# A relative attention bias laid out from 32 shifted lines a head in place of 128, and read as 256 columns in place of 384

## The chip, the cores and the metric

The kernel runs on one core of one Trainium2 chip. The metric is the device time of one execution in microseconds (us); lower is better. Five engines work side by side, each through its own instructions in order: TensorE (PE in the profile; its weight loads are listed as PEld), VectorE (DVE), ScalarE (ACT), GpSimd (POOL) and SyncE (SP), which here issues all the DMA transfers.

## The reference

One step of a two-layer streaming encoder for 256 prompt frames and 32 sample frames of width 1024. Only the start of layer 0 matters here. Half of its 16 heads (group A, 8 heads of size 64) attend to their own chunk of 64 frames and those before it, with a learned bias a head that depends on the clipped distance of query and key:

```python
def rel_bias_table(rel_bias, q_loc, k_loc):
    rel = jnp.clip(q_loc[:, None] - k_loc[None, :], -REL_CLIP, REL_CLIP) + REL_CLIP
    return jnp.moveaxis(rel_bias[rel].astype(jnp.float32), -1, 0)

def band_attend(q, k, v, bias, valid=None):
    s = jnp.einsum('bqhd,bkhd->bhqk', q, k).astype(jnp.float32) * (HEAD_DIM ** -0.5) + bias
    if valid is not None:
        s = jnp.where(valid, s, NEG_INF)
    p = jax.nn.softmax(s, axis=-1)
    return jnp.einsum('bhqk,bkhd->bqhd', p.astype(v.dtype), v)
```

The other eight heads (group B) use stick-breaking attention without a bias. Then follow the output projection, cross-attention into 256 memory rows, a SwiGLU block, and layer 1 with 16 forgetting-attention heads and the same two blocks.

## The kernel before

Activations lie with features on the partitions: eight tiles of 128 features by 288 tokens (256 prompt, 32 sample). A weight matrix comes in blocks of 128x1024, 512 KB each. `unit` loads one into `st` (a pool of four), ScalarE casts it to a high part `hi`, and VectorE subtracts to get the low part `lo`; `project` then runs 24 matmuls of 288 columns into one accumulator `pj`, three for each of the eight feature tiles: `hh` by `hi`, `hl` by `hi`, `hh` by `lo`. A projection can thus begin when `hi` is cast but needs `lo` from its third matmul on.

Layer 0's mixing (`mix_ab`) goes over eight pairs of heads, j = 0 to 7. For each pair it projects q, k and v in this order; I call them q0, k0, v0, q1 and so on. VectorE takes each out of its accumulator, scaled by `rstd` (`evac_q`, line 718; `evac_kv`, line 725), and k and v are also stored to memory (the transfer `kv<-kv`, line 726). Pairs 0 to 3 are group A. After v of a pair, `attend_prompt` (line 357) transposes v (`vt`), makes the scores (`sc`), runs `softmax` on VectorE and ScalarE (`e`), transposes the weights (`tp`, copied out as `pt`) and multiplies by v (`po`). After odd pairs the sample frames of two pairs are attended to as well (`ss`, `es`, `ts`, `os`).

The bias of a head is a line of 384 numbers, and query p reads it shifted by p. After q0, `rel_lines` (line 729) writes the eight lines to memory and copies each 128 times with a stride of 385 into `skew`; read back with a stride of 384, row p is the line shifted by p. `rel_prompt` (line 749) fetches a head's bias as a tile `bi` of 128x384: 128 columns for the first 128 queries against the first 128 keys, 256 for the second 128 queries against all 256, and fills the future chunk's two corners with a large negative number. `rel_sample` (line 757) fetches 32 rows of 160 columns for each of four heads (`bs`).

The Python order of the code isn't the order on the engines. A scheduler places each instruction on its engine's queue when it expects its inputs and buffers to be there, and from then on the queue is fixed: SP issues its transfers in that order, and one that waits for its data stands in front of those behind it. Transfers also take turns on eight completion semaphores, so that each waits for the one eight places ahead of it to have landed.

Of the kernel before, what the change touches and what calls it, by code (L numbers as in the profile page):

```python
# [8 lines left out]
F32 = mybir.dt.float32  # L9
# [6 lines left out]
P = 128  # L16
NT = 288
NP = 256
NS = 32
KT = 8  # L20
NEG = -1e30
# [5 lines left out]
def encoder_step(ctx: ExitStack, tc: tile.TileContext, a):  # L27
# [13 lines left out]
    dr = ctx.enter_context(tc.tile_pool(name="dr", bufs=1, space=bass.MemoryType.DRAM))  # L41
    V, S, G, T, DMA = nc.vector, nc.scalar, nc.gpsimd, nc.tensor, nc.sync
    cnt = [0]

    def name(s):
        cnt[0] += 1
        return f"{s}{cnt[0]}"

    def tok(s, dt=F32):
        return tk.tile([P, NT], dt, tag="t", name=name(s))  # L50

    def work(s):
        return wk.tile([P, 512], F32, tag="w", name=name(s))
# [4 lines left out]
    def small(s):  # L58
        return sm.tile([P, 8], F32, tag="s", name=name(s))
# [4 lines left out]
    def att(s):  # L64
        return ps.tile([P, 512], F32, tag="at", bufs=4, name=name(s))

    def mm(out, lhsT, rhs, start=True, stop=True):
        T.matmul(out, lhsT, rhs, start=start, stop=stop, skip_group_check=True)  # L68
# [82 lines left out]
    def project(src, h, n=NT, w=None, begun=None):  # L151
        if begun:
            w, p = begun
        else:
            w, p = w or unit(src), acc("pj")
        with tc.issue_after(warmed.ins):
            for k in range(BEGIN if begun else 0, KT):
                mm3(p[:, :n], w, k, h, k, k == 0, k == KT - 1)
        tick()
        return p  # L160
# [167 lines left out]
    def v_natural(v):  # L328
        p = att("vt")
        T.transpose(p[:, 0:128], v[:, 0:128], ident)  # L330
        T.transpose(p[:, 128:256], v[:, 128:256], ident)
        T.transpose(p[0:NS, 256:384], v[:, 256:288], ident)
        vn = wk.tile([P, 384], F32, tag="vn", bufs=5, name=name("vn"))
        S.copy(vn[:, 0:256], p[:, 0:256])
        S.copy(vn[0:NS, 256:384], p[0:NS, 256:384])
        return vn

    def softmax(s, cols, bias, out):

        n, rows = len(cols), out.shape[0]  # L340
        st = small("st")[0:rows]
        for i, (c0, c1) in enumerate(cols):
            mx, sm = st[:, i:i + 1], st[:, n + i:n + i + 1]
            if bias is None:
                V.tensor_reduce(mx, s[:, c0:c1], axis=mybir.AxisListType.X, op=ALU.max, negate=True)
                S.activation(out[:, c0:c1], s[:, c0:c1], AF.Exp, bias=mx, accum_out=sm)
            else:
                V.tensor_tensor_reduce(out=out[:, c0:c1], in0=s[:, c0:c1], in1=bias[:, c0:c1], scale=-1.0, scalar=3e38,
                                       op0=ALU.add, op1=ALU.min, accum_out=mx)
                S.activation(out[:, c0:c1], out[:, c0:c1], AF.Exp, bias=mx, scale=-1.0, accum_out=sm)  # L350
        V.reciprocal(st[:, 2 * n:3 * n], st[:, n:2 * n])
        for i, (c0, c1) in enumerate(cols):
            V.tensor_scalar(out[:, c0:c1], out[:, c0:c1], st[:, 2 * n + i:2 * n + i + 1], None, op0=ALU.mult)

    QT = [(0, 128), (128, 384)]

    def attend_prompt(q, k, v, vns, j, bias, oh, ol):

        vn = vns[j] = v_natural(v)
        e = []  # L360
        for hd in range(2):
            r = slice(64 * hd, 64 * hd + 64)
            s = att("sc")
            mm(s[:, 0:128], q[r, 0:128], k[r, 0:128])
            mm(s[:, 128:384], q[r, 128:256], k[r, 0:256])
            e.append(work("e"))
            softmax(s, QT, bias[hd], e[hd])
        yield 1
        w = []
        for hd in range(2):  # L370
            t = att("tp")
            T.transpose(t[:, 0:128], e[hd][:, 0:128], ident)
            T.transpose(t[:, 128:256], e[hd][:, 128:256], ident)
            T.transpose(t[:, 256:384], e[hd][:, 256:384], ident)
            w.append(work("pt"))
            S.copy(w[hd][:, 0:384], t[:, 0:384])
        yield 1
        prompt_pv(w, vn, oh, ol)

    def prompt_pv(w, vn, oh, ol):  # L380
        po = att("po")
        for hd in range(2):
            r = slice(64 * hd, 64 * hd + 64)
            mm(po[r, 0:256], vn[:, 64 * hd:64 * hd + 64], w[hd][:, 0:256], True, False)
            mm(po[r, 128:256], vn[:, 128 + 64 * hd:192 + 64 * hd], w[hd][:, 256:384], False, True)
        split_o(po[:, 0:256], oh[:, 0:256], ol[:, 0:256])
# [329 lines left out]
    def evac_q(cur, p):  # L716
        t = tok("q")
        cur.then(lambda: V.scalar_tensor_tensor(t, p[:, :NT], 0.125, cur.r, op0=ALU.mult, op1=ALU.mult))
        return t

    def evac_kv(cur, p, dst):
        t = tok("kv")

        def go():
            V.tensor_tensor(t, p[:, :NT], cur.r, ALU.mult)
            DMA.dma_start(dst, t)

        cur.then(go)
        return t

    def rel_lines():


        ln = cst.tile([8, 384], F32, name="line")
        DMA.dma_start(ln[:, 128:384], a["rel"][:, 0:256])
        V.tensor_copy(ln[:, 0:128], ln[:, 128:129].to_broadcast([8, 128]))
        d = dr.tile([8, 384], F32, name="lined")
        DMA.dma_start(d, ln)
        sk = dr.tile([8, 128 * 385], F32, name="skew")
        for h in range(8):  # L740
            DMA.dma_start(bass.AP(tensor=sk.tensor, offset=sk.offset + h * 128 * 385, ap=[[385, P], [1, 384]]),
                          bass.AP(tensor=d.tensor, offset=d.offset + 384 * h, ap=[[0, P], [1, 384]]))
        return sk

    def rel_rows(sk, h, c, rows, n):

        return bass.AP(tensor=sk.tensor, offset=sk.offset + h * 128 * 385 + c, ap=[[384, rows], [1, n]])

    def rel_prompt(sk, h):
        t = wk.tile([P, 384], F32, tag="bi", bufs=5, name=name("bi"))  # L750
        DMA.dma_start(t[:, 0:128], rel_rows(sk, h, 256, P, 128))
        DMA.dma_start(t[:, 128:384], rel_rows(sk, h, 128, P, 256))
        G.memset(t[0:64, 64:128], NEG)
        G.memset(t[0:64, 320:384], NEG)
        return t

    def rel_sample(sk, g):
        t = wk.tile([P, 384], F32, tag="bi", bufs=5, name=name("bs"))
        for h in range(4):
            DMA.dma_start(t[32 * h:32 * h + 32, 0:160], rel_rows(sk, 4 * g + h, 128, NS, 160))  # L760
        return t

    def mix_ab(cur, nxt, memory, w0):
        o = ([tok("oh", F32R) for _ in range(KT)], [tok("ol", F32R) for _ in range(KT)])
        qs, ks, vs, vns = {}, {}, {}, {}
        w = a["w_ab"]

        def proj(j):
            b = 12 * (j // 4) + j % 4
            kv = 8 * (j // 4) + j % 4  # L770
            qs[j] = evac_q(cur, project(w[b], cur.h, w=w0 if j == 0 else None))
            if j == 0:
                proj.line = rel_lines()
            ks[j] = evac_kv(cur, project(w[b + 4], cur.h), a["kv0"][kv])
            vs[j] = evac_kv(cur, project(w[b + 8], cur.h), a["kv0"][kv + 4])

        def attend(j):
            args = (qs[j], ks[j], vs[j], vns, j)
            if j < 4:
                return attend_prompt(*args, [rel_prompt(proj.line, 2 * j + i) for i in range(2)], o[0][j], o[1][j])  # L780
            return stick_prompt(*args, o[0][j], o[1][j])

        def sample(g):
            two = (2 * g, 2 * g + 1)
# [249 lines left out]
```

## Time and profile before

| what | value |
|---|---|
| median of 3 runs | 981.52 us (979.58 to 983.31) |
| the profiled execution | 981.77 us, span 979.9 us |
| TensorE busy, share of the span | 960.9 us, 98% |
| VectorE, ScalarE, GpSimd busy | 589.5, 483.8, 194.6 us |
| copies `skew<-lined` | 8 issues of 192 KB, 13.7 to 18.7 us, 6.5 us to landing |
| bias reads `bi<-skew` | 8 of 64 KB and 8 of 128 KB, 20.1 to 49.9 us |
| sample bias reads `bs<-skew` | 8 of 20 KB |

Busy time is the union of an engine's instructions. The bias is read in the first 50 us only, so the span's averages say little about it; the rows of that stretch count. In the timeline a row has start, duration, engine, line, operation, output and inputs, count, and in brackets the idle time ahead with what ended it. In the rows by stretch there are, after the stretch's bounds and length, the busy times of PE, PEld, DVE, ACT and POOL, then the granted TensorE clock, the DMA share and GB/s. A wait row names who waited and for whom, with the total, the count and the longest.

### The profile page before, as it was taken

Reading aid. Unit: us, or ns where it says so; the run is one execution under the profiler, and the core shown is the slowest. Engines: PE = TensorE matmul, PEld = TensorE weight load, DVE = VectorE, ACT = ScalarE, POOL = GpSimd, SP = SyncE. Lnnn points to the kernel's source line nnn. Section 1 sums busy time; section 2 is a strip of 40 time slices with the busy share of each in tenths; the row PEclk is TensorE's granted clock in tenths of the full one; section 3 lists DMA queues with packets and bytes.
Section 4 is the critical chain, followed back from the end, with each engine's and each line's share of the span. In section 5 each row is a group of like instructions: output and inputs, shape, how many; then the busy total and the mean of one; then the engine's idle time right before and its main releaser. Section 6 shows DMA issues by size and latency. Waiting matters only on the chain.

```text
span 979.9 us, 19034 instructions
## 1 busy us (share of the span) xinstructions
PE 960.9 (98%) x7449; PEld 925.1 (94%) x7449; DVE 589.5 (60%) x1135; ACT 483.8 (49%) x854; POOL 194.6 (20%) x293
## 2 busy tenths in 40 slices
PE   8999999999999999999999999999999999999995
PEld 7789999998899999999998999999989999999995
DVE  6686454677676555764565666657757655555452
ACT  5556767555455444444444545445546544444330
POOL 3121001210113222411003234213002222222010
PEclk9999999999999999999999999999999999999997
DMA  7775345544254454455455555545425444444431
GB/s 235 247 248 192 127 165 174 169 168 143 91 179 158 165 173 167 178 193 173 166 201 167 179 191 182 170 160 194 149 100 168 155 159 165 173 164 166 165 109 49
DMA packets 60137, 163.59 MB, mean 167 GB/s; under 512 B 8160, under 2 KB 21520, under 8 KB 60048
## 3 DMA queue, kind: packets, MB, share of 16 engines
q1 hardware_dynamic: 60048, 162.38, 49.0%
q8 instruction: 59, 0.97, 0.4%
q14 instruction: 30, 0.25, 0.1%
HBM read 152.20 MB, written 11.72 MB: 167 GB/s over the span
## 4 chain that ended last, share of the span: by engine, by line
PE 90%; DMA 3%; DVE 3%; issue 1%; ACT 1%; SPq 0%; POOL 0%; DVEq 0%; ACTq 0%; POOLq 0%
PE pj L68 50%; PE dn L68 14%; PE op L68 11%; PE mv L68 5%; DMA st<-w_ab 2%; PE zb L68 1%; PE xs L68 1%; PE xo L68 1%; PE po L68 1%; DVE lo L142 1%; DMA skew<-lined 1%; PE sc L68 1%; PE nr L68 1%; ACT hi L141 1%; PE zs L68 1%
## 5 line engine op out<-in xcount | busy, mean ns | idle before, releaser
L141 ACT CAST hi<-st 128x1024 fp32r<-128x1024 f32 x260 | 272.2, 1049 | 339.4 <-issue 146.9
L68 PE MATMUL pj<-hh,hi 128*128 128x288 f32 (+1 forms) x1352 | 405.1, 300 | 0.0
L68 PE MATMUL pj<-hl,hi 128*128 128x288 f32 (+1 forms) x1352 | 399.8, 296 | 1.7 <-DVE hl L248 1.7
L142 DVE TENSOR_TENSOR lo<-st,hi 128x1024 fp32r<-128x1024 f32 x260 | 323.3, 1244 | 128.8 <-PE dn L68 41.3
L68 PE MATMUL pj<-hh,lo 128*128 128x288 f32 (+1 forms) x1352 | 399.4, 295 | 0.0
L68 PEld LDWEIGHTS pj<-hh,hi 128*128 128x128 f32 x1352 | 256.6, 190 | 6.2 <-issue 4.7
L68 PEld LDWEIGHTS pj<-hl,hi 128*128 128x128 f32 x1352 | 256.5, 190 | 3.3 <-DVE hl L248 3.2
L68 PEld LDWEIGHTS pj<-hh,lo 128*128 128x128 f32 x1352 | 256.7, 190 | 0.0
L68 PE MATMUL dn<-fh,hi 128*128 128x288 f32 x400 | 108.7, 295 | 0.0
L68 PE MATMUL dn<-fh,lo 128*128 128x288 f32 x352 | 103.7, 295 | 0.0
L68 PE MATMUL dn<-fl,hi 128*128 128x288 f32 x304 | 89.5, 294 | 0.0
L68 PE MATMUL op<-ol,hi 128*128 128x288 f32 x256 | 75.5, 296 | 0.0
L68 PE MATMUL op<-oh,lo 128*128 128x288 f32 x256 | 75.5, 295 | 0.0
L68 PE MATMUL op<-oh,hi 128*128 128x288 f32 x256 | 75.1, 296 | 0.0
L68 PEld LDWEIGHTS dn<-fh,hi 128*128 128x128 f32 x400 | 72.5, 188 | 0.0
L68 PEld LDWEIGHTS dn<-fh,lo 128*128 128x128 f32 x352 | 66.1, 188 | 0.0
L213 POOL TENSOR_TENSOR ssq<-ssq,sq 128x288 f32<-128x288 f32 (+1 forms) x37 | 37.0, 1000 | 120.0 <-ACT sq L202 77.8
L68 PEld LDWEIGHTS dn<-fl,hi 128*128 128x128 f32 x304 | 57.1, 188 | 0.0
L691 POOL TENSOR_TENSOR fl<-us,fh 128x288 fp32r<-128x288 f32 x38 | 32.8, 863 | 119.0 <-ACT fh L690 119.0
L686 DVE TENSOR_TENSOR us<-pj,rstd 128x288 f32<-128x288 f32 x44 | 20.1, 457 | 59.4 <-PE pj L68 59.4
L687 POOL TENSOR_TENSOR gs<-gs,sg 128x288 f32<-128x288 f32 x44 | 38.8, 882 | 75.5 <-ACT sg L685 75.5
L68 PEld LDWEIGHTS op<-ol,hi 128*128 128x128 f32 x256 | 48.2, 188 | 0.8 <-issue 0.8
(253 smaller groups left out, 1213.7 us busy)
## 6 DMA issues: line engine op xcount, KB each, us to landing
st<-w_gate SPq DMA_DIRECT2D x44, 512.0 KB, 3.3
st<-w_up SPq DMA_DIRECT2D x44, 512.0 KB, 3.2
st<-w_down SPq DMA_DIRECT2D x44, 512.0 KB, 3.3
st<-w_c SPq DMA_DIRECT2D x25, 512.0 KB, 3.3
st<-w_ab SPq DMA_DIRECT2D x23, 512.0 KB, 4.2
st<-w_xk SPq DMA_DIRECT2D x16, 512.0 KB, 3.6
st<-w_xv SPq DMA_DIRECT2D x16, 512.0 KB, 3.5
st<-w_xq SPq DMA_DIRECT2D x16, 512.0 KB, 4.3
```

The lines of the kernel that those rows point to most:

```text
L68: T.matmul(out, lhsT, rhs, start=start, stop=stop, skip_group_check=True)
L141: S.copy(hi[:, b], st[:, b])
L142: V.tensor_tensor(lo[:, b], st[:, b], hi[:, b].bitcast(F32), ALU.subtract)
L213: eng.tensor_tensor(s[:, :self.n], self.acc[i][:, :self.n], q[:, :self.n], ALU.add)
L686: V.tensor_tensor(us, pu[:, :NT], cur.r, ALU.mult)
L687: G.tensor_tensor(gs, gs, sg, ALU.mult)
L691: G.tensor_tensor(lo, us, hi.bitcast(F32), ALU.subtract)
```

## The change

The shifted copies are made for 32 rows a head, by two transfers of four heads in place of eight of one. A head's bias is fetched by four transfers of 32 rows and 256 columns, each from a start 32 further left in the line. The tile then holds only the 256 columns of the second 128 queries; the first 128 queries use columns 128 to 255 of the same tile, since the same distances stand there, and one corner is filled in place of two.

```diff
-    def softmax(s, cols, bias, out):
+    def softmax(s, cols, bias, out, at=None):
...
-                V.tensor_tensor_reduce(out=out[:, c0:c1], in0=s[:, c0:c1], in1=bias[:, c0:c1], scale=-1.0, scalar=3e38,
+                b0 = at[i] if at else c0
+                V.tensor_tensor_reduce(out=out[:, c0:c1], in0=s[:, c0:c1], in1=bias[:, b0:b0 + c1 - c0], scale=-1.0, scalar=3e38,
...
-        sk = dr.tile([8, 128 * 385], F32, name="skew")
-        for h in range(8):
-            DMA.dma_start(bass.AP(tensor=sk.tensor, offset=sk.offset + h * 128 * 385, ap=[[385, P], [1, 384]]),
-                          bass.AP(tensor=d.tensor, offset=d.offset + 384 * h, ap=[[0, P], [1, 384]]))
+        sk = dr.tile([8, SKEW], F32, name="skew")
+        for h in range(0, 8, 4):
+            DMA.dma_start(bass.AP(tensor=sk.tensor, offset=sk.offset + h * SKEW, ap=[[SKEW, 4], [385, NS], [1, 384]]),
+                          bass.AP(tensor=d.tensor, offset=d.offset + 384 * h, ap=[[384, 4], [0, NS], [1, 384]]))
...
+    SKEW = NS * 385
+
+    def rel_rows(sk, h, c, n):
+
+        return bass.AP(tensor=sk.tensor, offset=sk.offset + h * SKEW + c, ap=[[384, NS], [1, n]])
...
     def rel_prompt(sk, h):
         t = wk.tile([P, 384], F32, tag="bi", bufs=5, name=name("bi"))
-        DMA.dma_start(t[:, 0:128], rel_rows(sk, h, 256, P, 128))
-        DMA.dma_start(t[:, 128:384], rel_rows(sk, h, 128, P, 256))
-        G.memset(t[0:64, 64:128], NEG)
-        G.memset(t[0:64, 320:384], NEG)
+        for p in range(0, P, NS):
+            DMA.dma_start(t[p:p + NS, 0:256], rel_rows(sk, h, 128 - p, 256))
+        G.memset(t[0:64, 192:256], NEG)
         return t
...
-                return attend_prompt(*args, [rel_prompt(proj.line, 2 * j + i) for i in range(2)], o[0][j], o[1][j])
+                return attend_prompt(*args, [rel_prompt(proj.line, 2 * j + i) for i in range(2)], o[0][j], o[1][j], (128, 0))
```

The scheduler then places the neighbours of these instructions anew, on all five queues, between the copies and about 70 us into the program; behind that the queues are as before. In the names below, numbers only tell tiles apart, and they differ by a few between the two kernels.

On SP, from v1's weights (`st_508`) to the store of k1 (`kv_505`), before; `st_568` is q2's weights, `kv_344` and `kv_385` are k0 and v0:

```order
L136 DMA st_508<-w_ab 128x1024
L751 DMA bi_549<-skew 128x128
L752 DMA bi_549<-skew 128x256
L726 DMA kv<-kv_344 128x288
L726 DMA kv<-kv_385 128x288
L751 DMA bi_554<-skew 128x128
L752 DMA bi_554<-skew 128x256
L502 DMA ca_559<-cab 128x512
L502 DMA ca_561<-cab 128x512
L760 DMA bs_563<-skew 32x160 x4
L136 DMA st_568<-w_ab 128x1024
L726 DMA kv<-kv_505 128x288
```

and now, where `st_504` is v1's weights, `st_566` q2's, `kv_501` k1 and `kv_542` v1:

```order
L727 DMA kv<-kv_338 128x288
L727 DMA kv<-kv_379 128x288
L756 DMA bi_382<-skew 32x256 x4
L756 DMA bi_388<-skew 32x256 x4
L727 DMA kv<-kv_501 128x288
L136 DMA st_504<-w_ab 128x1024
L756 DMA bi_545<-skew 32x256 x4
L756 DMA bi_551<-skew 32x256 x4
L503 DMA ca_557<-cab 128x512
L503 DMA ca_559<-cab 128x512
L727 DMA kv<-kv_542 128x288
L136 DMA st_566<-w_ab 128x1024
```

The stores of k0 and v0 moved ahead of the first bias reads, v1's weights moved behind the store of k1, and q2's weights, with k2's and v2's behind them, moved behind the store of v1. (Between the last `ca` and `kv_542` stand four reads of `bs` as before.)

On VectorE, the softmax of pair 0 before (`e_439` and `e_451` are its two heads; `kv_505`, k1, came after both):

```order
L142 TENSOR_TENSOR lo_511<-st_508,hi_510 128x1024
L348 ISA e_439,st_440<-sc_436,bi_388 128x128
L348 ISA st_440 128x1
L348 ISA e_439,st_440<-sc_436,bi_388 128x256
L348 ISA st_440 128x1
L348 ISA e_451,st_452<-sc_448,bi_393 128x128
L348 ISA st_452 128x1
L348 ISA e_451,st_452<-sc_448,bi_393 128x256
L348 ISA st_452 128x1
L351 RECIPROCAL st_440<-st_440 128x2
```

and now:

```order
L726 TENSOR_TENSOR kv_501<-pj_464,rstd_374 128x288
L349 ISA e_435,st_436<-sc_432,bi_382 128x128
L349 ISA st_436 128x1
L349 ISA e_435,st_436<-sc_432,bi_382 128x256
L349 ISA st_436 128x1
L352 RECIPROCAL st_436<-st_436 128x2
L354 TENSOR_SCALAR e_435<-e_435,st_436 128x128
L354 TENSOR_SCALAR e_435<-e_435,st_436 128x256
L349 ISA e_447,st_448<-sc_444,bi_388 128x128
```

k1's evacuation moved ahead of the softmax, and the second head begins only when the first is scaled; v1's low part comes after both.

On TensorE, the end of pair 1's scores for the sample frames before, with k2's projection (`pj_661`) behind it:

```order
L68 MATMUL ss_638<-ca_559,q_460 32x128
L68 MATMUL ss_638<-kv_505,q_460 32x32
L68 MATMUL pj_661<-hh_166,hi_657 128x288
L68 MATMUL pj_661<-hl_167,hi_657 128x288
L68 MATMUL pj_661<-hh_166,lo_658 128x288
```

and now, with q2's projection (`pj_572`) two matmuls into it:

```order
L68 MATMUL ss_636<-kv_501,q_456 32x32
L373 MATMUL tp_692<-ident,e_615 128x128
L374 MATMUL tp_692<-ident,e_615 128x128
L375 MATMUL tp_692<-ident,e_615 128x128
L373 MATMUL tp_698<-ident,e_627 128x128
L374 MATMUL tp_698<-ident,e_627 128x128
L375 MATMUL tp_698<-ident,e_627 128x128
L400 MATMUL ts_704<-ident,es_645 128x128
L401 MATMUL ts_704<-ident,es_645 32x128
L68 MATMUL po_752<-pt_696,vn_609 64x256
L68 MATMUL po_752<-pt_696,vn_609 64x128
L68 MATMUL pj_572<-hh_166,hi_568 128x288
```

Before, q2 stood ahead of the scores and k2 between scores and transposes; now q2, k2 and v2 stand together behind the transposes.

More of the change, by code (lines that the diff above doesn't have):

```diff
@@ L355, in encoder_step, with attend_prompt @@
     QT = [(0, 128), (128, 384)]
-    def attend_prompt(q, k, v, vns, j, bias, oh, ol):
+    def attend_prompt(q, k, v, vns, j, bias, oh, ol, at=None):
         vn = vns[j] = v_natural(v)
@@ L366, in attend_prompt @@
             e.append(work("e"))
-            softmax(s, QT, bias[hd], e[hd])
+            softmax(s, QT, bias[hd], e[hd], at)
         yield 1
@@ L738, in rel_lines @@
         DMA.dma_start(d, ln)
-        sk = dr.tile([8, 128 * 385], F32, name="skew")
-        for h in range(8):
-            DMA.dma_start(bass.AP(tensor=sk.tensor, offset=sk.offset + h * 128 * 385, ap=[[385, P], [1, 384]]),
-                          bass.AP(tensor=d.tensor, offset=d.offset + 384 * h, ap=[[0, P], [1, 384]]))
-        return sk
-    def rel_rows(sk, h, c, rows, n):
-        return bass.AP(tensor=sk.tensor, offset=sk.offset + h * 128 * 385 + c, ap=[[384, rows], [1, n]])
+        sk = dr.tile([8, SKEW], F32, name="skew")
+        for h in range(0, 8, 4):
+            DMA.dma_start(bass.AP(tensor=sk.tensor, offset=sk.offset + h * SKEW, ap=[[SKEW, 4], [385, NS], [1, 384]]),
+                          bass.AP(tensor=d.tensor, offset=d.offset + 384 * h, ap=[[384, 4], [0, NS], [1, 384]]))
+        return sk
+    SKEW = NS * 385
+    def rel_rows(sk, h, c, n):
+        return bass.AP(tensor=sk.tensor, offset=sk.offset + h * SKEW + c, ap=[[384, NS], [1, n]])
     def rel_prompt(sk, h):
         t = wk.tile([P, 384], F32, tag="bi", bufs=5, name=name("bi"))
-        DMA.dma_start(t[:, 0:128], rel_rows(sk, h, 256, P, 128))
-        DMA.dma_start(t[:, 128:384], rel_rows(sk, h, 128, P, 256))
-        G.memset(t[0:64, 64:128], NEG)
-        G.memset(t[0:64, 320:384], NEG)
+        for p in range(0, P, NS):
+            DMA.dma_start(t[p:p + NS, 0:256], rel_rows(sk, h, 128 - p, 256))
+        G.memset(t[0:64, 192:256], NEG)
         return t
@@ L759, in rel_sample @@
         for h in range(4):
-            DMA.dma_start(t[32 * h:32 * h + 32, 0:160], rel_rows(sk, 4 * g + h, 128, NS, 160))
+            DMA.dma_start(t[32 * h:32 * h + 32, 0:160], rel_rows(sk, 4 * g + h, 128, 160))
         return t
```

## The prediction

> **What bounds the kernel now.** I read the page first: the engine totals and the chain of work that ended last.
>
> ```profile
> PE 960.9 (98%) x7449; PEld 925.1 (94%) x7449; DVE 589.5 (60%) x1135; ACT 483.8 (49%) x854; POOL 194.6 (20%) x293
> ...
> PE 90%; DMA 3%; DVE 3%; issue 1%; ACT 1%; SPq 0%; POOL 0%; DVEq 0%; ACTq 0%; POOLq 0%
> ```
>
> TensorE is busy for 98% of the span and carries 90% of the chain, so a change is worth what it adds to or takes from TensorE's idle time. The DMA share of the chain is small and lies in the first 60 us, where the bias is made and read. So the next view is the engines' busy time between 17 us, when the projections run evenly, and 66 us, when the last of the eight biased heads has been transposed:
>
> ```profile
> 17.00:66.00 49.00, 46.36 (x371) 41.76 (x371) 34.77 (x101) 24.30 (x61) 7.03 (x21) 1.00 0.80 251
> ```
>
> The first number after the length is TensorE: 46.36 of 49.00 us. It idles 2.6 us there, and that is the most the change can give back: 981.5 - 2.6 = 978.9 us. The loss has no such limit, and the rest of the argument is about it.
>
> **What the weights wait for.** All transfers leave through SP, in its order. The timeline of SP:
>
> ```profile
> 13.65 5.05 SPq L741 DMA_DIRECT2D skew<-lined  x8
> ...
> 23.37 0.96 SPq L136 DMA_DIRECT2D st<-w_ab  x1
> ...
> 25.41 0.82 SPq L726 DMA_DIRECT2D kv<-kv  x2
> ...
> 28.76 1.82 SPq L760 DMA_DIRECT2D bs<-skew  x4
> 30.68 0.37 SPq L136 DMA_DIRECT2D st<-w_ab  x1
> 34.04 0.36 SPq L726 DMA_DIRECT2D kv<-kv  x1
> 34.49 0.38 SPq L525 DMA_DIRECT2D mem<-memT  x1
> 34.96 0.88 SPq L136 DMA_DIRECT2D st<-w_ab  x2
> ```
>
> The weights at 23.37 are v1's (the value projection of head pair 1), those at 30.68 q2's, the two at 34.96 k2's and v2's. They run ahead of the work: v1's weights leave 8 us before k1's projection has ended. The row at 34.04 is k1's result being stored; SP had nothing out for 3 us before it, and the three loads behind it follow at its heels. A store that waits for its data holds up what stands behind it.
>
> ```profile
> 28.47 0.40 PE L68 MATMUL pj<-hh,hi 128*128 128x288 f32 x1
> ...
> 31.62 0.29 PE L68 MATMUL pj<-hh,lo 128*128 128x288 f32 x1
> ...
> 33.53 0.30 PE L372 MATMUL tp<-ident,e 128*128 128x128 f32 x1 [0.27 <-DVE e L353]
> ...
> 33.89 0.38 PE L68 MATMUL pj<-hh,hi 128*128 128x288 f32 x1
> ...
> 37.27 0.88 PE L68 MATMUL po<-pt,vn 128*64 128x256 f32 x8
> ...
> 53.65 0.40 PE L68 MATMUL pj<-hh,hi 128*128 128x288 f32 x1
> ```
>
> This is TensorE before the change: k1 from 28.47 to 31.62 (24 matmuls, so 0.133 us from start to start), the softmax transposes, v1 from 33.89, the first value product at 37.27, and q3 at 53.65, after q2, k2 and v2. From q3 on the order is nearly the old one, so q3's start is where I read off the sum.
>
> **The change part by part.** Traffic: six of eight shifted copies go, at 5.05/8 = 0.63 us each 3.8 us of SP's time. The reads of the bias go from 16 issues to 32; at the 28.76 row's rate (1.82/4 = 0.46 us for transfers of 32 rows) the 16 more cost 7.4 us of SP's time. Eight fills of 64x64 on POOL go; POOL is busy 7.03 of the 49 us, so nothing is counted. The softmax reads its bias elsewhere in the tile and is otherwise the same, so nothing either. The wait that disappears:
>
> ```profile
> SPq L751 <- DMA skew<-lined: 1.9, 2, 1.4
> ```
>
> It was SP's, not TensorE's. What takes its place is in the order: with the copies finished early, the scheduler has put v1's weights behind the store of k1, and q2's, k2's and v2's weights behind the store of v1. The durations I need:
>
> ```profile
> 28.45 1.05 ACT L141 CAST hi<-st 128x1024 fp32r<-128x1024 f32 x1 [3.92 <-DMA st<-w_ab]
> ...
> 40.63 1.05 ACT L141 CAST hi<-st 128x1024 fp32r<-128x1024 f32 x1 [2.05 <-DMA st<-w_ab]
> ...
> 43.01 1.05 ACT L141 CAST hi<-st 128x1024 fp32r<-128x1024 f32 x1 [1.01 <-DMA st<-w_ab]
> ```
>
> ```profile
> 24.94 0.81 DVE L725 TENSOR_TENSOR kv<-pj,rstd 128x288 f32<-128x288 f32 x2
> ...
> 29.53 1.23 DVE L142 TENSOR_TENSOR lo<-st,hi 128x1024 fp32r<-128x1024 f32 x1 [1.68 <-ACT hi L141]
> 30.67 0.28 DVE L348 CUSTOM_DVE_ANT_0 e<-sc,bi 128x128 f32<-128x128 f32 x1
> ...
> 32.02 0.17 DVE L351 RECIPROCAL st<-st 128x2 f32<-128x2 f32 x1 [0.15 <-ACT e L350]
> 32.22 0.55 DVE L353 TENSOR_SCALAR e<-e,st 128x128 f32<-128x128 f32 x2
> ```
>
> ```profile
> st<-w_gate SPq DMA_DIRECT2D x44, 512.0 KB, 3.3
> ...
> st<-w_ab SPq DMA_DIRECT2D x23, 512.0 KB, 4.2
> ...
> bs<-skew SPq DMA_DIRECT2D x8, 20.0 KB, 3.7
> ```
>
> Nothing before k1's last matmul at 31.62 hangs on the change: its weights leave before the copies. From there, in the new order:
>
> - VectorE takes k1 out of PSUM when its last matmul ends (31.62 + 0.29), at 31.95. SP's store follows 0.47 later (24.94 to 25.41 in the rows): 32.42. v1's weights leave at 32.87. The queue is calm, so I take w_gate's 3.3 us: 36.17 (w_ab's 4.2 would give 37.1). In the old order they had left at 23.37.
> - The softmax of pair 0 now stands behind k1's evacuation on VectorE: 32.32 in place of 30.67. Its bias leaves SP after the stores at 25.41, eight issues of 0.46 from 26.28 on, the fourth at 27.7, landed by 31.4 at the 3.7 us of the small reads: in time. The second head now starts only when the first is scaled, 2.1 us later by the rows (30.67 to 32.22 + 0.55). Its scaling ends at 36.4, its transposes at 36.8. That ends with the weights, so it adds nothing to them.
> - Cast from 36.25, low half 1.08 later (28.45 to 29.53) and 1.23 long: 38.6. Then 22 of v1's matmuls: 41.5. Before, v1 and the product behind it were done at 38.1: **+3.4 us**.
> - v1's evacuation 41.74, its store 42.21, q2's weights 42.66, with three more loads at 43.1 (memory), 43.55 (k2) and 44.0 (v2). Meanwhile scores and softmax of pair 1, with no projection between scores and transposes: TensorE's next 22-matmul block needs q2's low half. Landing 46.0 to 46.8, cast behind a copy 46.7, low half 47.8 to 49.0, q2 done at 52.0.
> - k2's weights are third in that row. Before, loads at 34.49, 34.96 and 35.45 were ready at about 40.6 (second) and 43.0 (third, 7.5 us). So k2's land between 48.7 (1.3 us apart) and 51.0 (7.5 us); the late end makes TensorE wait 1.1 us for the low half. Then k2 and v2, 3.2 us each, and half of the sample product, 0.3: q3 at 58.75 to 59.8 against 53.65. **+5.1 to +6.1; I take +5.5.** The transposes' old waits of 2.6 us are replaced within this walk, not to be subtracted again.
>
> Later weights stand behind stores too, but k3, v3 and q4 find theirs landed when the walk is carried on (k2 done at 55.6, its store and one more load, v3's weights out by 57.5 and landed by 62; q3, scores and k3 keep TensorE until 67), and past 66 us TensorE's own work fills the span, so the delay is carried to the end.
>
> **The clock.** The idle stretch brings a second cost. The windows of 3.41 us by which the granted clock changes (last columns but two):
>
> ```profile
> 30.86:34.27 3.41, 2.41 (x17) 1.87 (x17) 2.80 (x15) 2.44 (x10) 0.00 (x0) 1.00 0.54 190
> ...
> 512.13:515.54 3.41, 2.30 (x18) 1.57 (x17) 1.91 (x8) 0.00 (x0) 0.00 (x0) 1.00 0.50 160
> 515.55:518.96 3.41, 3.41 (x18) 3.41 (x17) 1.99 (x4) 1.76 (x3) 0.79 (x2) 0.50 0.14 46
> 518.97:522.37 3.40, 3.40 (x29) 3.40 (x28) 1.56 (x2) 1.36 (x2) 1.09 (x2) 1.00 0.78 231
> ```
>
> After a window with TensorE busy 2.30 us the next was granted 0.50; after one with 2.41 it was not. The half-rate window passed 18 matmuls where the next passed 29, so a full one costs 3.41 x (1 - 18/29) = 1.3 us. In the new order TensorE has, between 31.9 and 38.6, six transposes (0.3 each), the value product (0.88) and two matmuls: 3 us at most in 6.7, so some window has well under 2.3, and v1 starts at half rate. I add **+1.3**; bounds 0 (the window ends just as v1 starts, or none counts) and 1.8 (v1's 2.9 us all at 18/29). A second such stretch, before q2 at 49, holds transposes and products closer together; 0 to 1.3 more, taken as 0.
>
> [...]
>
> **Sum.** +5.5 + 1.3 = +6.8. The profiled execution took 981.77 us (span 979.9 and 1.9 around it), 0.25 above the median of 981.52. From its own time 988.6; against the median **988.3 us**. A measurement of this kernel tells apart about 0.5%, 4.9 us.
>
> **Rivals.**
> 1. The walk without the clock's fall: 987.0. For it: the 2.41 row kept full rate. Against: the gap is twice as long. [...]
> 2. The clock falls twice, or v1's and k2's weights land late (4.2 and 7.5 us): 5.5 + 2.6 + up to 1.5, so 989.6 to 991.1. For it: the second stretch without projection between 46 and 49; against: denser work in it.
> 3. Not slower: SP does not really stand still at a store, so v1's weights leave at about 28 with the bias reads, land by 32, and TensorE goes on as before; with less traffic it then regains up to 2.6 us: 978.9 to 981.5. It decides at whether weights are cast before 32.5. For it: 0.80 of DMA time is in use there and much goes away. Against: the rows at 34.04 to 34.96.
>
> **Chances.** Forecast 0.45 (own range 986.5 to 989.5), rival 1 0.20, rival 2 0.17, rival 3 0.14, anything faster than 976.6 0.04, since no idle time of that size is there to be won. Rival 1 lies at the edge of 0.5% (986.4) and is split evenly: slower 0.45 + 0.17 + 0.10 = 0.72, same 0.14 + 0.10 = 0.24, faster 0.04. The range of 8 in 10 leaves out rival 3 and the far end of rival 2: 984.0 to 991.5.
>
> **What would show it.** v1's weights issued after 32 us, behind a store; their cast past 36; TensorE idle some 5 us more between 31.9 and 50 and q3 near 59 to 60; a granted clock of 0.50 for 3.4 us between 34 and 45; from q3 on the same distances as before. The forecast is wrong if v1's weights are cast by 33, or if q3 starts late and the end does not.

## The result and the profile after

The changed kernel takes **993.62 us** (median of 4 runs, 992.40 to 994.24) against 981.63 us for the kernel before in the same session: 1.0122 times as long, with a 95% interval of 1.0104 to 1.0141. It is 12.0 us slower. I had forecast 988.3 us (+6.8) with a range to 991.5. The direction and the place were right; the size was not, and the cause goes one step further back than I had looked.

The profiled execution took 993.16 us with a span of 991.4, 11.5 more than before. The page of the changed kernel, engine totals and chain:

```profile
PE 966.5 (97%) x7449; PEld 927.6 (94%) x7449; DVE 591.0 (60%) x1135; ACT 484.7 (49%) x854; POOL 192.3 (19%) x285
...
PE 93%; DVE 2%; DMA 1%; issue 1%; ACT 1%; SPq 0%; POOL 0%; DVEq 0%; ACTq 0%; POOLq 0%
```

TensorE is busy for 5.6 us more than before with the same 7449 matmuls, so some of them ran slower. The stretch from 17 to 66 us, by engine, which before held 46.36 us of TensorE work and 371 matmuls:

```profile
17.00:66.00 49.00, 42.58 (x297) 35.85 (x296) 25.03 (x74) 16.58 (x41) 3.10 (x9) 0.90 0.45 145
```

74 matmuls fewer were done by 66 us, and the mean granted clock was 0.90 in place of 1.00. SP's timeline there:

```profile
13.46 1.35 SPq L742 DMA_DIRECT2D skew<-lined  x2
24.67 0.82 SPq L727 DMA_DIRECT2D kv<-kv  x2
25.59 3.65 SPq L756 DMA_DIRECT2D bi<-skew  x8
31.70 0.36 SPq L727 DMA_DIRECT2D kv<-kv  x1
32.16 0.38 SPq L136 DMA_DIRECT2D st<-w_ab  x1
...
44.87 0.36 SPq L727 DMA_DIRECT2D kv<-kv  x1
45.33 0.38 SPq L136 DMA_DIRECT2D st<-w_ab  x1
```

The copies cost SP 1.35 us in place of 5.05, and then SP issues nothing for almost 10 us, from 14.8 to 24.67, because the next thing in its order is a store that waits for k0. v1's weights leave at 32.16 behind k1's store, q2's at 45.33 behind v1's. VectorE:

```profile
31.22 0.46 DVE L726 TENSOR_TENSOR kv<-pj,rstd 128x288 f32<-128x288 f32 x1 [4.11 <-PE pj L68]
31.59 0.28 DVE L349 CUSTOM_DVE_ANT_0 e<-sc,bi 128x128 f32<-128x128 f32 x1
...
33.60 0.28 DVE L349 CUSTOM_DVE_ANT_0 e<-sc,bi 128x128 f32<-128x128 f32 x1
...
37.38 1.23 DVE L142 TENSOR_TENSOR lo<-st,hi 128x1024 fp32r<-128x1024 f32 x1 [1.69 <-ACT hi L141]
```

It stood still for 4.11 us waiting for k1's last matmul, while the scores of pair 0 were ready (TensorE made them from 26.87 on, in 0.93 us) and the last of the first head's four bias pieces had landed at 28.66. The softmax then starts within 0.4 us of k1's evacuation: it waited for its place in the order and for nothing else. TensorE:

```profile
30.89 0.29 PE L68 MATMUL pj<-hh,lo 128*128 128x288 f32 x1
33.56 0.30 PE L373 MATMUL tp<-ident,e 128*128 128x128 f32 x1 [2.39 <-DVE e L354]
...
35.57 0.30 PE L373 MATMUL tp<-ident,e 128*128 128x128 f32 x1 [1.40 <-DVE e L354]
...
38.18 1.55 PE L68 MATMUL po<-pt,vn 128*64 128x128 f32 x6
39.66 0.61 PE L68 MATMUL pj<-hh,lo 128*128 128x288 f32 x1
...
44.05 0.29 PE L68 MATMUL pj<-hh,lo 128*128 128x288 f32 x1
...
48.42 0.30 PE L373 MATMUL tp<-ident,e 128*128 128x128 f32 x1 [1.68 <-DVE e L354]
...
54.03 0.40 PE L68 MATMUL pj<-hh,lo 128*128 128x288 f32 x1
...
63.73 0.40 PE L68 MATMUL pj<-hh,hi 128*128 128x288 f32 x1
```

The rows are the end of k1; the two heads' transposes, each waiting for VectorE; the value product; v1 without its first two matmuls (39.66 to 44.05; before, all 24 ran from 33.89 to 37.04); pair 1's transposes; the rest of q2; and q3, which began at 53.65 before. The stretches of 3.41 us by which the granted clock changes in this execution (the clock is the last column but two):

```profile
29.38:32.79 3.41, 1.80 (x14) 1.56 (x12) 1.01 (x5) 0.88 (x4) 0.15 (x1) 1.00 0.15 40
32.80:36.21 3.41, 1.25 (x6) 0.67 (x6) 1.98 (x10) 1.45 (x7) 0.00 (x0) 1.00 0.73 235
36.21:39.62 3.41, 3.18 (x12) 1.55 (x10) 1.23 (x1) 1.43 (x2) 0.29 (x2) 0.50 0.57 181
39.63:43.04 3.41, 3.41 (x15) 3.38 (x15) 0.42 (x1) 0.37 (x1) 0.00 (x0) 0.50 0.09 22
...
46.45:49.86 3.41, 1.56 (x22) 0.86 (x14) 3.14 (x18) 3.07 (x12) 0.00 (x0) 1.00 0.90 261
49.87:53.28 3.41, 3.41 (x11) 1.80 (x11) 2.27 (x5) 2.43 (x4) 0.00 (x0) 0.50 1.02 390
```

So the clock was at half from 36.21 to 43.04, 6.8 us, while the value product and most of v1 ran, and from 49.87 to 53.28, 3.4 us more, ahead of the rest of q2: three windows of 3.41 us, where I had counted one.

### The profile page after: what moved, and what is told of

Same layout as the page of the kernel before. It is cut to its first block, busy times and chain, and to the rows that moved or that the text cites. A ratio compares the mean times of both kernels' runs of the same rounds, so it can differ in the third digit from the quotient of the medians.

```text
span 991.4 us, 19047 instructions
## 1 busy us (share of the span) xinstructions
PE 966.5 (97%) x7449; PEld 927.6 (94%) x7449; DVE 591.0 (60%) x1135; ACT 484.7 (49%) x854; POOL 192.3 (19%) x285
## 4 chain that ended last, share of the span: by engine, by line
PE 93%; DVE 2%; DMA 1%; issue 1%; ACT 1%; SPq 0%; POOL 0%; DVEq 0%; ACTq 0%; POOLq 0%
PE pj L68 52%; PE dn L68 14%; PE op L68 10%; PE mv L68 5%; PE po L68 2%; PE zb L68 1%; PE xs L68 1%; PE xo L68 1%; PE sc L68 1%; PE nr L68 1%; PE zs L68 1%; PE nrm L68 1%; DMA x<-xT 1%; PE xss L68 1%; PE xso L68 1%
```

## The experiments

All are timed against the kernel before on the same chip. Theories: **A**, the loss is the order of the queues, with the fall of the clock as its consequence; **B**, the loss is the transfers themselves (reads of 32 rows, twice as many of them, and the copies); **C**, it is TensorE's order alone. The first four kernels start from the changed one: two put back one order each, one puts back both, and one adds dummy matmuls.

**SP's order put back.** The stores of k and v of pairs 0 to 3 are issued three weight loads later.

```diff
+            if hold:
+                held.append(lambda: DMA.dma_start(dst, t))
...
+            if held and len(held) > 2:
+                with tc.issue_after(load.ins):
+                    held.pop(0)()
```

> The changed kernel, but the stores of k and v of pairs 0 to 3 stand three weight loads later on SP, so that no weights wait behind them; TensorE's order stays that of the changed kernel. Theory A (both queues' orders cost time, SP's and TensorE's, and the clock falls in the gaps): v1's weights leave before 30 us, but v1 still stands behind the transposes and the value product, and q2, k2, v2 behind those of pair 1, so about half of the 12 us comes back: 985 to 989. Theory B (the 32-row transfers themselves are what is slow, whatever the order): 992 to 994. Theory C (only TensorE's order matters, the weights' place on SP does not): 992 to 994.

Measured: 991.83 us, ratio 1.0104 (1.0089 to 1.0119). v1's weights left at 23.81, 8 us earlier than in the changed kernel, and yet the first transposes ran at 33.70 and v1, but for its first two matmuls, from 39.86 to 43.77. A's bracket was missed by almost 3 us: early weights alone change little. VectorE's softmax still stood behind k1, and v1's low half behind the softmax, done at 37.62; and TensorE still had the value product ahead of v1's third matmul; the 21 steps from there on took 3.91 us in place of 21 x 0.133 = 2.79.

**TensorE's order put back.** Attention steps of pairs 0 to 3 are held behind the last matmul of the projection that they follow in the code.

```diff
+        if rest_after:
+            with tc.issue_after(last.ins):
+                tick()
```

> The changed kernel, but TensorE's order in pairs 0 to 3 is that of the kernel before (scores, transposes and products each behind the projection ahead of them); SP still has v1's weights behind the store of k1. Theory A: v1 starts at about 37.5 where it was 33.9, q2 some 3 us late too, and the clock may fall once: 984 to 988. Theory B: 991 to 994. Theory C: 980 to 983.

Measured: 994.25 us, 1.0125 (1.0110 to 1.0141), the time of the changed kernel. C is out, A's bracket was missed by 6 us, and the time lies just above B's.

**Both together.**

> The changed kernel with both: the stores three loads later on SP, and TensorE's old order in pairs 0 to 3. Theory A: all of the loss is gone, 979 to 982, and granted clock 1.00 between 20 and 60 us. Theory B: the loss stays to a good part, 987 to 994. Theory C: 980 to 983, no lower than with TensorE's order alone.

Measured: 989.89 us, 1.0081 (1.0066 to 1.0096). A third of the loss came back, A was missed again, by 8 us, and the time lies in B's bracket. VectorE in this kernel shows what was not put back:

```profile
31.32 0.46 DVE L735 TENSOR_TENSOR kv<-pj,rstd 128x288 f32<-128x288 f32 x1 [4.10 <-PE pj L68]
31.69 0.28 DVE L358 CUSTOM_DVE_ANT_0 e<-sc,bi 128x128 f32<-128x128 f32 x1
...
33.70 0.28 DVE L358 CUSTOM_DVE_ANT_0 e<-sc,bi 128x128 f32<-128x128 f32 x1
...
36.35 1.23 DVE L147 TENSOR_TENSOR lo<-st,hi 128x1024 fp32r<-128x1024 f32 x1 [0.56 <-ACT hi L146]
```

With weights and bias early, VectorE still waits 4.10 us for k1, takes one head after the other, and makes the low half of v1's weights last. So A had to be widened: the scheduler had laid out *every* queue for a bias that it held to be late, and freeing two of them leaves the third in charge. Up to here this is an argument from the order, and B is still open.

**The clock kept up in the changed kernel**, with 72 dummy matmuls ahead of pair 0's first transpose.

> The changed kernel with 72 needless 128-column matmuls ahead of pair 0's first transpose, in the gap after k1's projection (their result is overwritten). They add no work on the path if done by about 35 us. If the half-rate stretch from 36.2 to 43.0 us is what makes v1 and the product before it late (theory A's clock term), it is gone and q3 starts 2 to 3 us earlier: 990 to 992. If the clock costs only the 1.3 us of the prediction: 992 to 992.5. If the clock does not matter there: 993.6, or up to 994.5 with the added matmuls in the way.

Measured: 993.29 us, 1.0126 (1.0105 to 1.0147). The dummies ended at 36.15 and themselves delayed the first transpose to 35.98 (33.56 in the changed kernel), so this run doesn't tell, although q3 started at 62.71 in place of 63.73; the cleaner one comes below.

What in the change makes the scheduler plan for a late bias? The next four look for it.

**Eight copies in place of two**, all else of the change kept:

```diff
-        for h in range(0, 8, 4):
-            DMA.dma_start(bass.AP(..., ap=[[SKEW, 4], [385, NS], [1, 384]]),
-                          bass.AP(..., ap=[[384, 4], [0, NS], [1, 384]]))
+        for h in range(8):
+            DMA.dma_start(bass.AP(..., ap=[[385, NS], [1, 384]]),
+                          bass.AP(..., ap=[[0, NS], [1, 384]]))
```

> The changed kernel with one difference: its shifted lines are written by eight copies, one a head of 32 lines, in place of two copies of four heads each. The reads stay as they are (four of 32 rows and 256 columns a head). Written this way the scheduler keeps v1's weights ahead of k1's store on SP and the softmax of pair 0 ahead of k1's evacuation on VectorE, as in the kernel before. Theory A (the loss is the order of all queues, which the four-head copies set off): 979 to 983 us, v1 under way before 35 us, q3 before 55 us. Theory B (the small reads themselves: 32 issues in place of 16, more descriptors): 988 to 994 us, as with the change whole. Theory C (the clock falls whatever the order is, since transposes still wait): v1 at half rate, 983 to 986 us.

Measured: **983.28 us against 982.52, ratio 1.0010 (0.9999 to 1.0021)**. The whole loss is gone, with every 32-row read still there. B is out for the reads. SP and TensorE of this kernel:

```profile
13.96 4.99 SPq L742 DMA_DIRECT2D skew<-lined  x8
19.00 4.81 SPq L756 DMA_DIRECT2D bi<-skew  x8
23.91 0.37 SPq L136 DMA_DIRECT2D st<-w_ab  x1
25.33 0.83 SPq L727 DMA_DIRECT2D kv<-kv  x2
```

```profile
31.55 0.29 PE L68 MATMUL pj<-hh,lo 128*128 128x288 f32 x1
31.86 0.30 PE L373 MATMUL tp<-ident,e 128*128 128x128 f32 x1
...
32.88 0.38 PE L68 MATMUL pj<-hh,hi 128*128 128x288 f32 x1
...
53.85 0.40 PE L68 MATMUL pj<-hh,hi 128*128 128x288 f32 x1
```

v1's weights leave ahead of the stores, the transposes follow k1 without a wait, and q3 starts at 53.85 (before 53.65).

**Two four-head copies in the old kernel**, the reverse:

```diff
-        for h in range(8):
+        for h in range(0, 8, 4):
             DMA.dma_start(...)   # four heads of 128 lines each
```

> The kernel before with one difference, the reverse of the run above: its 128 shifted lines a head are written by two copies of four heads each in place of eight. All reads and the 128 lines stay. The scheduler now puts v1's weights behind k1's store on SP and the softmax of pair 0 behind k1's evacuation on VectorE, though less of the rest moves than in the changed kernel. Theory A: v1's weights leave after 31 us and v1 starts 3 us or more late, at half rate or not: 984 to 991 us. Theory B: nothing in it has 32 rows that had not before, so 980 to 983 us.

Measured: 992.70 us, 1.0106 (1.0085 to 1.0126): a loss, as A had it and B not, but 1.7 us above A's upper end. And this run has a second cause: with 128 lines a head the two copies are four times as large, and the bias really was late. The first softmax started at 35.78, behind a fill of the bias tile that had waited for its transfer, so the run alone does not tell order from data.

**256 columns alone**, with the old 128 lines and eight copies, one read a head:

```diff
-        DMA.dma_start(t[:, 0:128], rel_rows(sk, h, 256, P, 128))
-        DMA.dma_start(t[:, 128:384], rel_rows(sk, h, 128, P, 256))
+        DMA.dma_start(t[:, 0:256], rel_rows(sk, h, 128, 256, P))
```

> One half of the change alone: 256 columns of the bias are read a head in one read of 128 rows, in place of 128 and 256 columns in two, and one corner is filled in place of two; the 128 shifted lines and their eight copies stay as in the kernel before. Theory A: the order on TensorE is nearly that of before (6 places differ), so the time is too: 979 to 982 us, the lower end if the transposes of the first pairs wait less. Theory B: the same, since no 32-row read is added. A time above 985 us would put the loss on the read of 256 columns, against both.

Measured: 982.04 us, ratio 0.9994 (0.9985 to 1.0004). No change, and none could be expected beyond the 2.6 us that TensorE idled there. In its profiled execution q3 did start early, at 52.15 for 53.65, but that was gone by the end (982.06 us for 981.77).

**The late order forced on the old kernel.** Bias, copies and reads as before; only v1's weights are queued behind k1's store and q2's, k2's and v2's behind v1's.

```diff
+        if behind is not None:
+            with tc.issue_after(behind):
+                w, p = unit(src), acc("pj")
```

> The kernel before, its bias and all its transfers unchanged, with only an order forced: v1's weights are queued behind k1's store on SP, and q2's, k2's and v2's behind v1's store; the scheduler lays the other queues out around that. Theory A: the loss appears without any change to the bias, 986 to 993 us, with v1 after 37 us and q3 after 58 us. Theory B: the order costs no more than 1 us, 980 to 983 us.

Measured: 995.29 us, 1.0128 (1.0110 to 1.0146). The loss appears without touching the bias, as A said and against B; the time is 2.3 us above A's upper end. v1's weights left at 32.86, behind k1's store, and q2's at 46.32, behind v1's store. The softmax wasn't late here, pair 0's transposes ran at 31.08, so the place of the weights on SP, with the other queues laid out around it, is enough. TensorE's stretches in this kernel:

```profile
34.27:37.68 3.41, 0.00 (x0) 0.00 (x0) 0.00 (x0) 0.33 (x1) 0.00 (x0) 0.63 0.62 204
37.68:41.10 3.42, 2.24 (x8) 1.90 (x9) 1.23 (x1) 0.72 (x1) 0.00 (x0) 0.50 0.02 5
41.10:44.51 3.41, 3.41 (x16) 3.41 (x16) 0.00 (x0) 0.00 (x0) 0.00 (x0) 0.50 0.00 0
```

v1 ran at half rate from its first matmul to its last, 0.24 us from start to start in place of 0.133. How much of the loss is the clock? Two runs fill TensorE's waits with dummy matmuls that end before the work behind them can start.

**Forced order, with TensorE kept busy** (72 dummies behind pair 0's value product):

```diff
+        if busy.n == 1:
+            keep_busy(72, last)
```

> The old kernel with the forced order, and with 72 small dummy matmuls (128x128, their result unused) put on TensorE behind pair 0's value product, where it waits 5.07 us for v1's weights. They should take some 4.7 us and end before v1 starts at 38.45, so they cost nothing by themselves. Theory A with the clock: v1 ran at half rate throughout in the run without them (22 matmuls of 0.24 us in place of 0.133), so v1 ends 2.4 us earlier and the time falls by 1.5 to 3 us against the forced order alone, to 992 to 994 us. Rival (the clock's fall is hidden, because v1's successors wait for something else): no change, 995 to 996 us.

**Changed kernel, waits filled** (36 dummies behind k1, 20 behind the first head's transposes):

```diff
+        if fill:
+            keep_busy(fill, last)
...
+            if j == 0 and hd == 0:
+                keep_busy(20, last)
```

> The changed kernel with 36 dummy matmuls behind k1's last matmul and 20 behind the first head's transposes, in the two waits of 2.55 and 1.61 us; they should end before the transposes that follow. Theory A with the clock: no half-rate window between 36 and 43 us, the value product and v1 end 2.5 us earlier, the time falls by 1.5 to 3 us to 990.5 to 992.5 us; the other 9 to 10 us stay, since they are waits. Rival (the clock is the main loss): 984 to 988 us. Rival (no part in it): 993 to 994 us.

In the traces both did what they should. The same stretches of the forced order with dummies:

```profile
34.27:37.68 3.41, 2.96 (x53) 2.78 (x50) 0.03 (x1) 0.22 (x1) 0.00 (x0) 1.00 0.58 190
37.68:41.10 3.42, 2.17 (x17) 1.92 (x18) 1.22 (x1) 0.82 (x1) 0.00 (x0) 1.00 0.00 0
41.10:44.51 3.41, 2.86 (x24) 2.41 (x24) 0.46 (x1) 0.35 (x2) 0.00 (x0) 1.00 0.03 10
```

The clock stayed at 1.00, and q3 started at 60.94 in place of 65.31, with k1 ending at 31.00 and 30.94: **4.4 us** for the clock, which without dummies was at half for 10.2 us up to 45.37 and for 6.8 us more from 48.79 on. In the changed kernel q3 came at 61.49 in place of 63.73 although k1 ended 0.6 us later: 2.8 us, with one half-rate window left at 47 (mean clock 0.87 in the stretch from 44.51 to 47.92, 0.64 in the next). The times confirm this only in part. The forced order went from 995.29 to 992.53, inside A's bracket, but its runs spread from 989.37 to 997.23 and the interval, 1.0080 to 1.0143, overlaps that of the run without dummies. The changed kernel stayed at 993.73 (990.63 to 996.36), where A had 990.5 to 992.5: a miss. Why dummies widen the spread was not settled. The mean granted clock of the five runs of the forced order goes from 0.992 at 989.37 us, the one that was profiled, to 0.985 at 997.23, so others lost more of it; but 0.989 stands beside both 990.91 and 994.85.

**Four copies of two heads:**

```diff
-        for h in range(0, 8, 4):
+        for h in range(0, 8, 2):
```

> The changed kernel with its shifted lines written by four copies of two heads each, half way between the two copies of the change and the eight of the run that lost nothing. The scheduler still lays v1's weights behind k1's store, and the softmax of pair 0 behind k1's evacuation. Theory A (the order decides): 988 to 994 us, near the changed kernel's. Rival (the loss follows how long the copies themselves take): half of it, 985.5 to 988 us.

Measured: 992.93 us, 1.0113 (1.0088 to 1.0138): nearly the full loss, not half. It goes with the order, which is the late one here too. Nor were these copies half way between: they were still moving at 25 us, at 47 GB/s (last section), where the two of the change had ended by 21, so the loss does not grow with their time either.

**The change whole, its two copies issued by ScalarE:**

```diff
-            DMA.dma_start(bass.AP(tensor=sk.tensor, ...
+            nc.scalar.dma_start(bass.AP(tensor=sk.tensor, ...
```

> The changed kernel, with its two four-head copies and all its reads, but the two copies issued from ScalarE's queue in place of SP's. The scheduler then lays v1's, q2's and further weights ahead of the stores on SP, and the softmax of pair 0 ahead of k1's evacuation on VectorE, as in the kernel before. ScalarE waits for the line to land before it issues them, and casts q1's weights behind them, so q1 can start up to 2.5 us late. Theory A (the order of the queues): 979 to 985 us, with q3 before 57 us. Rival (the four-head copies or the 32-row reads cost the time themselves, by the transfers and not by the order): 988 to 994 us, as with the change whole. Between 985 and 988 us: both have a part.

Measured: 993.38 us, 1.0117 (1.0100 to 1.0133), against A's 979 to 985. Here ScalarE's queue became the trap. The waits of this kernel between 10 and 80 us:

```profile
ACT rstd L278 <- DMA skew<-lined: 11.4, 1, 11.4
```

ScalarE did no work for 11.4 us, until 26.84, with its second copy issued at 20.14 in between. The row puts the wait down to a copy, but the work behind it, `rstd`, also needs six matmuls of TensorE that ended at 26.80, so which came last is not settled. q1's cast stood behind it, so q1 started 4.3 us late, at 28.23, and ran at 0.24 us from start to start until 34.4, and a cast that waited 3.9 us for weights stood ahead of most of pair 0's exponentials. The transposes ran at 43.77. I had allowed 2.5 us for the first of these and nothing for the second. The time lies in the rival's bracket, but by this trace it is another way to lose the same 11 us, and decides nothing between A and B. So one more was made.

**The good kernel with two unread copies.** Eight copies make the bias, as in the run that lost nothing; two more in the four-head form, behind them, go to a place that nothing reads.

```diff
+        unused = dr.tile([8, SKEW], F32, name="unused")
+        for h in range(0, 8, 4):
+            DMA.dma_start(bass.AP(tensor=unused.tensor, ..., ap=[[SKEW, 4], [385, NS], [1, 384]]),
+                          bass.AP(tensor=d.tensor, ..., ap=[[384, 4], [0, NS], [1, 384]]))
```

> The kernel with eight copies of one head, which lost nothing, and behind them two further copies in the form of the change (four heads each) into a place that nothing reads. The bias itself is written and landed as in the run that lost nothing. The scheduler takes the two unread copies as something that holds up what follows on SP: v1's weights stand behind k1's store again, and the softmax of pair 0 behind k1's evacuation. Theory A (the order alone, whatever the data do): 989 to 995 us. Rival (the four-head copies cost time because the bias that they write arrives late): 981 to 984 us, since nothing waits for the unread ones.

Measured: 992.50 us, 1.0108 (1.0091 to 1.0125), inside A's bracket. SP and VectorE of this kernel:

```profile
18.87 1.34 SPq L746 DMA_DIRECT2D unused<-lined  x2
24.84 0.82 SPq L727 DMA_DIRECT2D kv<-kv  x2
...
31.87 0.36 SPq L727 DMA_DIRECT2D kv<-kv  x1
32.33 0.38 SPq L136 DMA_DIRECT2D st<-w_ab  x1
```

```profile
31.39 0.46 DVE L726 TENSOR_TENSOR kv<-pj,rstd 128x288 f32<-128x288 f32 x1 [4.11 <-PE pj L68]
31.76 0.28 DVE L349 CUSTOM_DVE_ANT_0 e<-sc,bi 128x128 f32<-128x128 f32 x1
```

It is the changed kernel's picture again. The longest of SP's own waits between 12 and 50 us:

```profile
SPq L727 <- DVE kv L726: 10.1, 2, 5.2
```

SP stands still for the stores' data, 10.1 us in two waits, and nothing waits for the two copies. The data were there, and still 11 us are lost. So the loss needs no late data: with the four-head copies on SP the scheduler lays out all queues as if for late transfers, and the chip then waits for the order. Two further copies in the one-head form were not tried behind the eight; that it is the form, and not only two more transfers, rests on the changed kernel against the one with eight copies. That the scheduler's belief is about how long such a copy takes is inferred from the orders, not measured.

No version beat the kernel before: eight copies with 32 lines, and 256 columns with 128 lines, both measure the same as it.

## Why the prediction was right in direction and wrong in size

- **The mechanism.** Weights behind stores, the softmax behind k1's evacuation, one head after the other: all as forecast, in the order's own sequence, and at the forecast times at first. v1's weights were cast at 36.30 (forecast 36.25), their low half was done at 38.61 (38.6). Two errors cancelled in this: the execution ran 0.7 us ahead at k1 (30.89 for 31.62), and the weights took 4.1 us from issue to cast (3.4).
- **The clock, the step that failed.** I counted one window, +1.3, and took a second stretch "as 0". Measured: three windows, 6.8 us in one piece and 3.4 us later. What they cost is worked out from the rows. v1's 21 steps took 4.39 us in place of 21 x 0.133 = 2.79, so 1.6; ahead of them the value product, at half rate too, held TensorE until 39.66, 1.05 us after the low half was ready, where I had let v1 start at once; and from pair 1's transposes to the rest of q2 passed 5.61 us (48.42 to 54.03), against 4.12 in the forced order with dummies at full clock, so 1.5 more. That is about 4.1 for 1.3. Rival 2 had the second fall, at 0.17, and only 2.6 for both.
- **The row behind it.** I read one window from the rows at 512: after a window with TensorE busy for 2.30 us came one at half rate, filled with work, and then full rate. In the changed kernel the clock fell after a window with 1.25 us (32.80 to 36.21), and the half-rate window behind it, busy for 3.18 of 3.41 us, was followed by a second. In the forced order three came in one piece: 0.63, 0.50, 0.50 and 0.87 in four stretches from 34.27 are 10.2 us at half. Nor is it the busy share alone that decides, as I had read it: the window at 29.38, with 1.80 us, was not followed by half rate, and neither was this one of the changed kernel:

```profile
524.32:527.73 3.41, 2.29 (x19) 1.51 (x17) 2.39 (x7) 0.43 (x1) 0.00 (x0) 1.00 0.44 133
527.74:531.15 3.41, 3.41 (x30) 3.41 (x30) 2.44 (x6) 1.43 (x3) 0.46 (x1) 1.00 0.37 117
```

  TensorE did not stand idle throughout ahead of the fall either: it was busy for 1.25 of the 3.41 us. Rival 1, the walk without the clock's fall (987.0), failed with these windows. After which windows the clock falls, and for how many, stays open.
- **q3.** Forecast 59.15 and 1.3 for the clock, so 60.45; measured 63.73. v1 ended at 44.3, 1.5 us after the forecast with its clock term; from there to the rest of q2 passed 9.7 us in place of 7.5; then q2, k2 and v2 took 9.7 in place of 10.15, since the wait for k2's weights that I had half counted did not come. Together the 3.3 us.
- **"From q3 on the same distances."** Not quite: +10.1 at q3, +11.5 at the end. The matmuls between 300 and 420 us stood a little further apart: from 320 to 400 us the kernel before did 608, the changed kernel 599, and 9 fewer are 1.2 us. The kernel with 256 columns alone also did 599 there, and its time is that of before, so I put this down to the execution and not to the change. Against it, the profiled execution of the kernel before lost 1.3 us to its half-rate window at 515.55, and the changed one, in the rows above, had none there. The two nearly cancel; where the remaining 1.4 us lie was not followed up.
- **Rival 3** (SP does not stand still) fell: SP stood still for almost 10 us at the first store.
- **Traffic.** SP saved 3.7 us on the copies and nothing came of it, as forecast; the 32 small reads cost nothing that stands clear of the spread (eight copies: 1.0010, at most 1.0021).
- **What I did not ask.** I took the new order from the build and costed it, and never asked which of the three edits had set it off. One build with eight copies would have shown that the order, and so the forecast, hung on how the copy is written.

## What to carry to other kernels

When a scheduler sets the order, a change of a transfer's *shape* can move every queue, and the cost is then in the order and not in the transfer: split a change into its edits and look which one moves the order before costing anything. A plan laid out for a late transfer was not mended here by freeing one queue: several queues hold the late plan, and freeing two of them recovered a third of the loss. A stretch with waits on TensorE can be lost twice, by the wait and by a half-rate clock: in these traces half rate lasted one to three windows of 3.41 us at a time, though not every such stretch brought it (the window behind the one at 29.38, with TensorE busy for 1.80 us, kept 1.00).

## What was not expected of the hardware

Half rate lasted 6.8 us in one piece in the changed kernel and 10.2 us in the forced order, two and three windows of 3.41 us. A window nearly full of work did not always end it: in the changed kernel the half-rate window from 36.21, with TensorE busy for 3.18 of 3.41 us, was followed by another; the second, from 39.63 and busy for all 3.41, was the last.

Copies of different form moved at different rates. By stretch, each with next to nothing else under way (the last two columns are the busy share of the DMA engines and GB/s): the changed kernel with its two copies of four heads, the run with four copies of two heads, and the kernel before with its eight copies of one head:

```profile
17.00:21.00 4.00, 4.00 (x34) 4.00 (x33) 3.74 (x11) 1.11 (x2) 0.00 (x0) 1.00 0.26 87
```

```profile
17.00:25.00 8.00, 8.00 (x64) 7.99 (x64) 5.36 (x17) 1.97 (x4) 0.00 (x0) 1.00 0.14 47
```

```profile
17.40:20.00 2.60, 2.60 (x25) 2.60 (x23) 2.36 (x3) 1.02 (x1) 0.00 (x0) 1.00 0.85 256
```

The four-head copies moved 87 GB/s at a busy share of 0.26, the two-head copies of the same lines 47 GB/s at 0.14, and the copies of the kernel before, which have 128 lines a head in place of 32, 256 GB/s at 0.85. The share is the mean over 16 DMA engines, so this is as much work as 4.2, 2.2 and 13.6 of them do when busy throughout; how it was spread over the engines, and why, was not shown. With 32 lines a head the slow form stays hidden: in the changed kernel DMA was at rest (share 0.00) from 21 to 25 us, before the first bias read at 25.59. With 128 lines, in the old kernel, DMA moved 88 to 109 GB/s from 17.0 to 26.6 us, and the bias was held back until after 35 us: the first fill of its tile, which waits for the read, ran at 35.59.
